# Gate of a feed-forward layer in pairs of blocks, by seven products of quarters

## The chip, the core and the metric

One core of a Trainium2 chip runs one program. The metric is the device time of one execution in microseconds, the median of several runs.

## The reference

Three transformer blocks in float32 on 256 tokens of 2048 features: two of a first kind (a state-space mixer beside latent attention, cross attention to a memory, feed-forward) and one hybrid block. What matters here is the feed-forward, with hidden width 5632:

```python
def swiglu(h, w_gate, w_up, w_down):
    return (jax.nn.silu(h @ w_gate) * (h @ w_up)) @ w_down
```

and the vector that shifts, scales and gates the hybrid block, a product of one row `c` with `w_ada` of 2048 x 6144:

```python
    ada = c @ w_ada + b_ada
    shift, scale, gate = jnp.split(ada, 3, axis=-1)
    h = rms_norm_2(x, g_pre) * (1.0 + scale[:, None, :]) + shift[:, None, :]
```

`shift` and `scale` are needed at the hybrid block's start, `gate` at its end.

## The kernel before, in words

Activations are kept feature-major as pairs of a high and a low part (`pair`, `hi_lo`, L348 to L370), four pairs of [128 features, 4 chunks, 256 tokens] for the 2048 features. A long product is computed in float32r as three matmuls: high x high, high x low of the weights, low x high (L423 to L425). `block` (L414) makes a token-major block of 512 columns: two PSUM banks of [128 tokens, 512], one for each token tile m, from the pool `psw` of four banks. Its weights come in half-tiles of [128, 2 chunks, 512], 512 KB each: `split` (L407) has SP load one into a `raw` buffer (five of them, L410), ACT copy it to `wh` (L411) and VectorE (DVE) subtract to get `wl` (L412). There are four `wh` and four `wl` buffers. A half-tile serves two chunks for both token tiles, 12 matmuls; the last half-tile of a block serves bank 0, then bank 1 (HOLD).

PE runs its instructions in the order in which the program is written; a scheduler orders those of the other engines by readiness and priority at build time, and each engine then runs its own in order. `early` (L316) and `weights` raise the priority. Work beside the long products is written as tasks (`spawn`, L265) that a `block` advances one step with every `tick` (L270), once for each chunk: the transposes of a hidden tile, attention heads and the like. A block of 2048 features has 15 ticks.

`ffn` (L1180) goes over 11 hidden blocks j of 512 columns in each of two layers: a gate block with Silu (L1188), an up block multiplied onto it (L1192), the transposes of the result as a task (L377, L358, L359), and the four down blocks of block j - 1, added to x by DVE (`x_add`, L485). In the second layer `ada` (L1234) then takes nine of 96 parts of `w_ada`: SP loads 512 KB into a slot, and DVE multiplies and sums it (L1240). `hybrid` (L1555) computes the last block, with four `ma` blocks beside which nothing else is loaded than their weights.

SBUF pools: `rawp` 5, `wp` 4, `xp` 6 pairs, and 72 KB a partition in `sp`, `k2`, `k1` for what tasks need. PSUM: four wide banks (`psw`) and four for the tasks (`psm`).

## Time and profile before

| | us |
|---|---|
| median of three runs | 3197.23 |
| lowest and highest run | 3197.22, 3197.4 |
| span of the profiled execution, first to last instruction | 3196.7 |
| first feed-forward stage | 454 to 1190 |
| second feed-forward stage | 1632 to 2360 |

The profile gives the span of the profiled execution; what lies around it, taken against the median, is 0.5 us. In the rows PE is TensorE's matmul queue, PEld its weight loads, DVE VectorE, ACT ScalarE, POOL GpSimd, SP the queue that issues most transfers. A matmul's record is longer than its spacing, since matmuls overlap.

### The profile page before, as it was taken

What the parts mean: (1) busy time and instruction counts of PE and PEld (TensorE: products, weight loads), DVE (VectorE), ACT (ScalarE), POOL (GpSimd) and SP (SyncE); (2) the same over time, 40 slices, a digit from 0 to 9 for tenths busy, and PEclk for the clock granted to TensorE, in tenths of its full rate; (3) what the DMA queues carried; (4) which work ended last, traced back from release to release, by engine and by line L of the source; (5) the groups of instructions that cost most, each with busy time, mean ns of one, the idle gap of its engine ahead of it and who ended that gap; (6) DMA issues with size and microseconds to landing.
All of it is one profiled execution on the core that took longest, in us unless ns stands there. A gap on an engine that the chain in (4) does not pass through costs nothing.

```text
span 3196.7 us, 41513 instructions
## 1 busy us (share of the span) xinstructions
PE 3175.3 (99%) x15705; PEld 2656.9 (83%) x15705; DVE 2034.1 (64%) x3015; ACT 1553.8 (49%) x2191; POOL 53.4 (2%) x77
## 2 busy tenths in 40 slices
PE   9999999999999999999999999999999999999998
PEld 8987888888888889887888888888878977888887
DVE  6886665555555566885767677766765555455554
ACT  7465564444444455474654444444454455444443
POOL 0010000000000000010000000000000000000000
PEclk9999999999999999999999999999999999999999
DMA  8554555555555556454567777777746533555454
GB/s 299 172 169 145 186 172 187 192 192 191 192 187 192 191 175 189 159 183 141 190 228 265 266 270 270 253 250 269 269 143 219 174 105 99 179 184 180 162 184 151
DMA packets 175160, 625.28 MB, mean 196 GB/s; under 512 B 19696, under 2 KB 19952, under 8 KB 174704
## 3 DMA queue, kind: packets, MB, share of 16 engines
q1 hardware_dynamic: 173952, 620.26, 58.2%
q8 instruction: 123, 2.02, 0.3%
q10 hardware_dynamic: 1008, 2.37, 0.2%
q14 instruction: 77, 0.63, 0.1%
HBM read 620.46 MB, written 2.10 MB: 195 GB/s over the span
## 4 chain that ended last, share of the span: by engine, by line
PE 96%; DVE 1%; DMA 1%; issue 1%; POOL 0%; ACT 0%; SPq 0%; DVEq 0%; POOLq 0%; ACTq 0%
PE pw L423 27%; PE pw L425 27%; PE pw L424 27%; PE pw L461 2%; PE pw L462 2%; PE pw L463 2%; PE mb L377 2%; PE mb L665 2%; DMA wada<-w_ada 1%; PE mb L1493 1%; PE mb L1346 0%; PE mb L903 0%; DVE wl L412 0%; PE mb L1496 0%; PE mb L887 0%
## 5 line engine op out<-in xcount | busy, mean ns | idle before, releaser
L412 DVE TENSOR_TENSOR wl<-raw,wh 128x1024 fp32r<-128x1024 f32 (+3 forms) x1069 | 1285.6, 1204 | 969.7 <-ACT wh L411 967.2
L411 ACT ACTIVATE wh<-raw 128x1024 fp32r<-128x1024 f32 (+3 forms) x1069 | 1114.9, 1043 | 1384.8 <-PE pw L425 1258.0
L423 PE MATMUL pw<-wh,xh 128*128 128x512 f32 (+2 forms) x3952 | 1555.4, 394 | 6.2 <-ACT wh L411 4.9
L425 PE MATMUL pw<-wh,xl 128*128 128x512 f32 (+2 forms) x3952 | 1526.3, 386 | 0.0
L424 PE MATMUL pw<-wl,xh 128*128 128x512 f32 (+2 forms) x3952 | 1524.6, 386 | 0.6 <-DVE wl L412 0.6
L423 PEld LDWEIGHTS pw<-wh,xh 128*128 128x128 f32 x3952 | 744.2, 188 | 153.3 <-ACT wh L411 4.9
L425 PEld LDWEIGHTS pw<-wh,xl 128*128 128x128 f32 x3952 | 743.1, 188 | 150.7 <-DVE xl L368 0.7
L424 PEld LDWEIGHTS pw<-wl,xh 128*128 128x128 f32 x3952 | 744.6, 188 | 141.6 <-DVE wl L412 2.1
L461 PE MATMUL pw<-xh,wh 128*128 128x256 f32 x640 | 183.2, 286 | 0.0
L463 PE MATMUL pw<-xh,wl 128*128 128x256 f32 x640 | 181.2, 283 | 0.0
L462 PE MATMUL pw<-xl,wh 128*128 128x256 f32 x640 | 181.1, 283 | 0.0
L485 DVE TENSOR_TENSOR x<-x,pw 128x512 f32<-128x512 f32 x224 | 144.9, 679 | 3.8 <-PE pw L425 3.8
L1240 DVE CUSTOM_DVE_ANT_0 wada<-wada,crow 128x1024 f32<-128x1024 f32 x96 | 117.3, 1221 | 33.9 <-DMA wada<-w_ada 33.8
L461 PEld LDWEIGHTS pw<-xh,wh 128*128 128x128 f32 x640 | 122.7, 192 | 1.3 <-issue 0.8
L462 PEld LDWEIGHTS pw<-xl,wh 128*128 128x128 f32 x640 | 122.8, 192 | 0.1
L463 PEld LDWEIGHTS pw<-xh,wl 128*128 128x128 f32 x640 | 122.7, 192 | 0.0
L630 ACT ACTIVATE t<-t,mn 128x256 f32<-128x256 f32 (+1 forms) x128 | 58.4, 457 | 63.1 <-DVE mn L627 62.3
L367 ACT ACTIVATE xh<-mb,par 128x256 fp32r<-128x256 f32 x112 | 50.9, 467 | 13.1 <-PE mb L377 12.2
L368 DVE SCALAR_TENSOR_TENSOR xl<-mb,par,xh 128x256 fp32r<-128x256 f32 x112 | 51.8, 478 | 3.7 <-ACT xh L367 2.6
L334 POOL TENSOR_TENSOR xr<-rs,mhalf 128x1 f32<-128x1 f32 x16 | 9.8, 619 | 2512.1 <-DVE rs L330 2306.4
L358 ACT ACTIVATE xh<-mb 128x512 fp32r<-128x512 f32 (+1 forms) x68 | 35.1, 516 | 30.5 <-PE mb L377 15.8
L627 DVE CUSTOM_DVE_ANT_0 t<-mb,cst 128x128 f32<-128x128 f32 x80 | 26.0, 354 | 25.8 <-PE mb L665 25.4
(358 smaller groups left out, 1564.4 us busy)
## 6 DMA issues: line engine op xcount, KB each, us to landing
raw<-w_gate SPq DMA_DIRECT2D x176, 512.0 KB, 3.6
raw<-w_up SPq DMA_DIRECT2D x176, 512.0 KB, 3.8
raw<-w_down SPq DMA_DIRECT2D x176, 512.0 KB, 3.6
raw<-w_out SPq DMA_DIRECT2D x96, 512.0 KB, 3.5
wada<-w_ada SPq DMA_DIRECT2D x96, 512.0 KB, 5.5
raw<-w_in_x SPq DMA_DIRECT2D x48, 512.0 KB, 3.9
raw<-w_in_z SPq DMA_DIRECT2D x32, 512.0 KB, 3.5
raw<-w_ma SPq DMA_DIRECT2D x32, 512.0 KB, 3.3
```

Source lines behind the costliest of these rows:

```text
L377: self.nc.tensor.transpose(t[:, j, m * P:(m + 1) * P], src(m), self.ident)
L411: nc.scalar.activation(h, raw, AF.Copy)
L412: nc.vector.tensor_tensor(l, raw, h.bitcast(F32), op=OP.subtract)
L423: nc.tensor.matmul(pt[m], lhsT=xh[:, k, ms], rhs=wh[:, j], start=c == 0, stop=False)
L424: nc.tensor.matmul(pt[m], lhsT=xh[:, k, ms], rhs=wl[:, j], start=False, stop=False)
L425: nc.tensor.matmul(pt[m], lhsT=xl[:, k, ms], rhs=wh[:, j], start=False, stop=c == 4 * n - 1)
L461: nc.tensor.matmul(pt, lhsT=h[:, j], rhs=xh[:, c], start=(k == 0), stop=False)
L462: nc.tensor.matmul(pt, lhsT=h[:, j], rhs=xl[:, c], start=False, stop=False)
L463: nc.tensor.matmul(pt, lhsT=l[:, j], rhs=xh[:, c], start=False, stop=(k == 15))
L485: self.nc.vector.tensor_tensor(xs, xs, pt[m], op=OP.add)
L665: nc.tensor.matmul(s[:, a:b], lhsT=q[:, m * P:(m + 1) * P], rhs=k[:, 0:b - a], start=(i == 0), stop=(i == len(parts) - 1))
L1240: nc.vector.tensor_tensor_reduce(out=t, in0=t, in1=self.crow[hf], scale=1.0, scalar=0.0, op0=OP.mult, op1=OP.add, accum_out=self.adap[:, j ...
```

## The change

Two gate blocks are computed together as a 2 x 2 by 2 x 2 product of quarters: the rows are the two token tiles, the contraction is the two halves of 1024 features, the columns are the two blocks. Seven products take the place of eight. Each has eight chunks of 128 features, for 128 tokens and 512 columns. The sums of activations are made once per layer (`x_sums`) and kept as high and low parts; the sums of weights are made anew for each pair: W00 + W01 and W11 + W01 by transfers from POOL that add to the tile in SBUF, the two later ones by additions on DVE. Block 0 is computed as before, blocks 1 to 10 in five pairs. A task, `gate_pair`, has 28 steps of one half-tile and six matmuls each, spread over 48 or 64 ticks of the two up blocks of the pair and the down blocks of the pair before. Down takes two hidden blocks in one PSUM accumulation.

The pools `sp`, `k2`, `k1` are closed for the feed-forward and give place to 70 KB a partition of others: `fs` (sums of activations, 8), `fr` (gate weights, 5), `fu` (up, 2), `fe` (temporaries, 4), `fc` (a row of `c`, 1). Each pair keeps one wide PSUM bank and up to three of the others.

`w_ada` is read in 96 transfers of two half rows into `raw` buffers: 7 at the start of each layer's feed-forward, 6 (first layer) or 4 (second) beside each pair, the last third, needed only for `gate`, beside the `ma` blocks of the hybrid block.

```diff
-    o["c_rows"] = np.ascontiguousarray(_rows(a["c_2"][0])).reshape(P, 2, 1024)
-    o["w_ada"] = np.ascontiguousarray(a["w_ada_2"][0].T).reshape(48, P, 2, 1024)
+    o["c_rows"] = np.ascontiguousarray(_rows(a["c_2"][0])).reshape(P, 4, 512)
+    w = a["w_ada_2"][0].T.reshape(24, 2, P, 4, 512)
+    o["w_ada"] = np.ascontiguousarray(w.transpose(0, 3, 2, 1, 4))
...
         self.tasks = []
         pool = lambda name, bufs, **k: ctx.enter_context(tc.tile_pool(name=name, bufs=bufs, **k))
         self.one = pool("one", 1)
+        self.sm = pool("sm", 1)
         self.rawp = pool("rawp", 5)
         self.wp = pool("wp", 4)
         self.xp = pool("xp", 6)
-        self.sp = pool("sp", NSLOT)
-        self.k2 = pool("k2", NT2)
-        self.k1 = pool("k1", NT1)
-        self.sm = pool("sm", 1)
         self.psw = pool("psw", 4, space=PSUM)
         self.psm = pool("psm", 4, space=PSUM)
+        self.scope = ctx.enter_context(ExitStack())
+        self.open_main()
         ctx.enter_context(tc.manual_schedule(engines={mybir.EngineType.PE}))
...
+    def part(self, **bufs):
+        self.scope.close()
+        for name, n in bufs.items():
+            setattr(self, name, self.scope.enter_context(self.tc.tile_pool(name=name, bufs=n, reuse_waits="tile")))
+    def open_main(self):
+        self.part(sp=NSLOT, k2=NT2, k1=NT1)
+    def open_ffn(self):
+        self.part(fs=8, fr=5, fu=2, fe=4, fc=1)
...
+    def half(self):
+        return self.fe.tile([P, 512], F32, name="fe", tag="fe")
+    def x_sums(self, pairs):
+        nc = self.nc
+        for t in pairs:
+            if isinstance(t, _Task):
+                yield from self.after(t)
+        prs = [self.get(t) for t in pairs]
+        S = [[self.fs.tile([P, 8, P], F32R, name="fs", tag="fs") for _ in range(2)] for _ in range(4)]
+        for i in range(2):
+            def quarter(k, m):
+                return [t[:, :, m * P:(m + 1) * P].bitcast(F32) for t in prs[2 * k + i]]
+            (h11, l11), (h12, l12), (h21, l21), (h22, l22) = (quarter(k, m) for m in range(2) for k in range(2))
+            def tmp():
+                return self.half().rearrange("p (a b) -> p a b", a=4)
+            flat = lambda t: t.rearrange("p a b -> p (a b)")
+            def put(n, t, sign=1.0):
+                h, l = (x[:, i * 4:i * 4 + 4] for x in S[n])
+                nc.scalar.activation(h, t, AF.Copy, scale=sign)
+                nc.vector.scalar_tensor_tensor(flat(l), flat(t), sign, flat(h.bitcast(F32)),
+                                               op0=OP.mult, op1=OP.subtract)
+            a, b = tmp(), tmp()
+            nc.vector.tensor_tensor(a, h21, h22, op=OP.subtract)
+            nc.vector.tensor_tensor(b, l21, l22, op=OP.subtract)
+            nc.vector.tensor_tensor(a, a, b, op=OP.add)
+            put(0, a, -1.0)
+            nc.vector.tensor_tensor(b, a, h11, op=OP.subtract)
+            nc.vector.tensor_tensor(b, b, l11, op=OP.subtract)
+            put(1, b)
+            c = tmp()
+            nc.vector.tensor_tensor(c, h12, b, op=OP.add)
+            nc.vector.tensor_tensor(c, c, l12, op=OP.add)
+            put(3, c, -1.0)
+            a, b = tmp(), tmp()
+            nc.vector.tensor_tensor(a, h11, h21, op=OP.subtract)
+            nc.vector.tensor_tensor(b, l11, l21, op=OP.subtract)
+            nc.vector.tensor_tensor(a, a, b, op=OP.add)
+            put(2, a)
+            yield 2
+        return S
+    def gate_pair(self, pairs, sums, srcs, r, u, ticks):
+        nc = self.nc
+        S = yield from self.after(sums)
+        pr = [self.get(t) for t in pairs]
+        def quarter(k, m):
+            return lambda c: [t[:, c % 4, m * P:(m + 1) * P] for t in pr[2 * k + c // 4]]
+        def total(n):
+            return lambda c: [t[:, c] for t in S[n]]
+        def load(k, n, q, t=None):
+            src = srcs[n][2 * k + q // 2][q % 2]
+            with self.early():
+                if t is None:
+                    t = self.fr.tile([P, 2, 512], F32, name="fr", tag="fr")
+                    nc.sync.dma_start(t, src)
+                else:
+                    nc.gpsimd.dma_start(t, src, accum_op=OP.add)
+            return t
+        def product(bank, x, t, q, first, last):
+            with self.early():
+                h = self.wp.tile([P, 2, 512], F32R, name="wh", tag="wh")
+                l = self.wp.tile([P, 2, 512], F32R, name="wl", tag="wl")
+                nc.scalar.activation(h, t, AF.Copy)
+                nc.vector.tensor_tensor(l, t, h.bitcast(F32), op=OP.subtract)
+            for j in range(2):
+                xh, xl = x(2 * q + j)
+                g = not first
+                nc.tensor.matmul(bank, lhsT=xh, rhs=h[:, j], start=first and q == 0 and j == 0, stop=False,
+                                 skip_group_check=g)
+                nc.tensor.matmul(bank, lhsT=xh, rhs=l[:, j], start=False, stop=False, skip_group_check=g)
+                nc.tensor.matmul(bank, lhsT=xl, rhs=h[:, j], start=False, stop=last and q == 3 and j == 1,
+                                 skip_group_check=g)
+        def gated(t, n, m, r=r):
+            while len(u) <= n:
+                yield 1
+            with self.early():
+                nc.scalar.activation(t, t, AF.Silu, scale=r[:, m:m + 1])
+                nc.vector.tensor_tensor(u[n][:, m], u[n][:, m], t, op=OP.mult)
+        def add(t, x):
+            with self.early():
+                nc.vector.tensor_tensor(t, t, x, op=OP.add)
+        done = [0]
+        def step():
+            done[0] += 1
+            return done[0] * ticks // 28 - (done[0] - 1) * ticks // 28
+        ba, bb, bd = self.wbank([P, 512]), self.bank([P, 512]), self.bank([P, 512])
+        ws = []
+        for q in range(4):
+            ws.append(load(0, 0, q))
+            product(ba, quarter(0, 0), ws[q], q, True, True)
+            load(0, 1, q, ws[q])
+            yield step()
+        for q in range(4):
+            product(bb, quarter(1, 0), load(1, 0, q), q, True, True)
+            yield step()
+        for q in range(4):
+            product(bd, total(0), ws[q], q, True, True)
+            yield step()
+        with self.early():
+            t1, t5 = self.half(), self.half()
+            nc.scalar.activation(t1, ba, AF.Copy)
+            nc.vector.tensor_tensor(t1, t1, bb, op=OP.add)
+            nc.scalar.activation(t5, bd, AF.Copy)
+        gate_1 = self.spawn(gated(t1, 0, 0), 1)
+        bc, be = self.bank([P, 512]), self.bank([P, 512])
+        for g in (0, 2):
+            a, b = {}, {}
+            for q in (g, g + 1):
+                a[q] = load(1, 1, q)
+                product(bd, total(3), a[q], q, False, True)
+                load(0, 1, q, a[q])
+                yield step()
+            for q in (g, g + 1):
+                product(bc, total(2), a[q], q, True, True)
+                b[q] = load(0, 0, q)
+                add(b[q], a[q])
+                yield step()
+            for q in (g, g + 1):
+                product(ba, total(1), b[q], q, False, True)
+                a[q] = load(1, 0, q)
+                add(a[q], b[q])
+                yield step()
+            for q in (g, g + 1):
+                product(be, quarter(1, 1), a[q], q, True, True)
+                yield step()
+        with self.early():
+            nr = self.small([P, 2], name="nr", bufs=1)
+            nc.vector.tensor_scalar(nr, r, -1.0, None, op0=OP.mult)
+            t2, t3 = self.half(), self.half()
+            nc.scalar.activation(t2, ba, AF.Copy)
+            nc.vector.tensor_tensor(t3, t2, bd, op=OP.add)
+            nc.vector.tensor_tensor(t2, t2, bc, op=OP.add)
+            nc.vector.tensor_tensor(t5, t2, t5, op=OP.add)
+            nc.vector.tensor_tensor(t2, t2, be, op=OP.add)
+        yield from gated(t3, 1, 0, nr)
+        yield from gated(t5, 1, 1, nr)
+        yield from gated(t2, 0, 1)
+        yield from self.after(gate_1)
     def ffn(self, l, pairs, r):
         nc, I = self.nc, self.I
         parts = self.x_parts()
-        def hidden(j):
-            s = self.slot([P, 2, 512], "ff")
-            pt = self.block(pairs, I["w_gate"][l, j])
+        last = l == DEPTH - 1
+        self.open_ffn()
+        self.crow = None
+        sums = self.spawn(self.x_sums(pairs), 1)
+        def up(j):
+            pt = self.block(pairs, I["w_up"][l, j])
+            s = self.fu.tile([P, 2, 512], F32, name="fu", tag="fu")
             for m in range(2):
-                nc.scalar.activation(s[:, m], pt[m], AF.Silu, scale=r[:, m:m + 1])
+                with self.early():
+                    nc.scalar.activation(s[:, m], pt[m], AF.Identity, scale=r[:, m:m + 1])
+            return s
+        def hidden(s, delay, first=None):
+            def steps():
+                if first is not None:
+                    yield from self.after(first)
+                return (yield from self.transposed(lambda m: s[:, m]))
+            return self.spawn(steps(), delay)
+        def down(js, hs):
+            for nb in range(4):
+                self.x_add(nb, self.block(list(hs), [I["w_down"][l, nb, j] for j in js]))
+                self.tick()
+        self.spawn(self.ada_steps(7, 4), 2)
+        s = up(0)
+        pt = self.block(pairs, I["w_gate"][l, 0])
+        for m in range(2):
+            t = self.half()
+            with self.early():
+                nc.scalar.activation(t, pt[m], AF.Silu, scale=r[:, m:m + 1])
+                nc.vector.tensor_tensor(s[:, m], s[:, m], t, op=OP.mult)
+        prev = [0], [hidden(s, 2)]
+        for js in ([1, 2], [3, 4], [5, 6], [7, 8], [9, 10]):
+            end = js[1] == NH_FFN - 1
+            u = []
+            srcs = [I["w_gate"][l, j] for j in js]
+            gate = self.spawn(self.gate_pair(pairs, sums, srcs, r, u, 48 if js[0] == 1 or end else 64), 1)
+            self.spawn(self.ada_steps(6 if l == 0 else 4, 8), 4)
+            for j in js:
+                u.append(up(j))
+            hs = [hidden(s, 1 + 4 * i, gate) for i, s in enumerate(u)] if end else None
+            down(*prev)
+            self.get(gate)
+            prev = js, hs or [hidden(s, 1 + 4 * i) for i, s in enumerate(u)]
+        js, hs = prev
+        if last:
+            self.ada_end()
+        out = []
+        for nb in range(4):
+            pt = self.block(hs, [I["w_down"][l, nb, j] for j in js])
+            if nb == 0:
+                self.open_main()
+            if nb == 3:
+                with self.tc.high_priority(offset=2 * HP):
+                    self.x_add(nb, pt, parts)
+                    r = self.x_rms(parts)
+            else:
+                self.x_add(nb, pt, parts)
+            out.append(self.spawn(self.x_fm(nb), 2) if last else self.x_pair(nb, self.p(f"{l + 1}.attn_g")))
             self.tick()
...
-    def ada_start(self):
-        nc = self.nc
...
-    def ada(self, n):
-        nc = self.nc
-        for i in self.ada_left[:n]:
-            j, hf = i // 2, i % 2
-            t = self.slot([P, 1024], "wada")
-            nc.sync.dma_start(t, self.I["w_ada"][j, :, hf])
-            nc.vector.tensor_tensor_reduce(
-                out=t, in0=t, in1=self.crow[hf], scale=1.0, scalar=0.0, op0=OP.mult, op1=OP.add,
-                accum_out=self.adap[:, j, hf:hf + 1])
+        return out, r
+    def ada(self, n, pool=None):
+        nc = self.nc
+        for k, i in self.ada_left[:n]:
+            if self.crow is None or self.crow[0] != k:
+                t = self.fc.tile([P, 512], F32, name="crow", tag="fc") if pool is None else pool([P, 512])
+                nc.sync.dma_start(t, self.I["c_rows"][:, k])
+                self.crow = k, t
+            t = self.rawp.tile([P, 2, 512], F32, name="raw", tag="raw")
+            nc.sync.dma_start(t, self.I["w_ada"][i, k])
+            for h in range(2):
+                nc.vector.tensor_tensor_reduce(
+                    out=t[:, h], in0=t[:, h], in1=self.crow[1], scale=1.0, scalar=0.0, op0=OP.mult, op1=OP.add,
+                    accum_out=self.adap[:, 2 * i + h, k:k + 1])
         self.ada_left = self.ada_left[n:]
+    def ada_steps(self, n, every, pool=None):
+        for _ in range(n):
+            with self.early():
+                self.ada(1, pool)
+            yield every
+    def ada_sum(self, lo, hi):
+        nc = self.nc
+        c = self.adac[:, lo:hi]
+        for t in [self.adap[:, lo:hi, k] for k in (1, 2, 3)] + [self.p("b_ada")[:, lo:hi]]:
+            nc.vector.tensor_tensor(c, c, t, op=OP.add)
     def ada_end(self):
         nc = self.nc
-        self.ada(96)
-        self.adac = self.one.tile([P, 48], F32, name="adac")
-        nc.vector.tensor_tensor(self.adac, self.adap[:, :, 0], self.adap[:, :, 1], op=OP.add)
-        nc.vector.tensor_tensor(self.adac, self.adac, self.p("b_ada"), op=OP.add)
+        self.ada(len(self.ada_left))
+        self.ada_sum(0, 32)
         self.g2 = self.one.tile([P, 16], F32, name="g2")
         nc.vector.scalar_tensor_tensor(self.g2, self.adac[:, 16:32], 1.0, self.p("g_pre"), op0=OP.add, op1=OP.mult)
+        self.ada_left = [(k, i) for k in range(4) for i in range(16, 24)]
...
+        self.crow = None
+        ada = self.spawn(self.ada_steps(32, 2, self.t2), 1)
...
+        self.get(ada)
         gr = self.spawn(self.gate_rows(), 2)
...
     def run(self):
-        self.ada_left = []
+        self.adap = self.one.tile([P, 48, 4], F32, name="adap")
+        self.adac = self.adap[:, :, 0]
+        self.crow = None
+        self.ada_left = [(k, i) for k in range(4) for i in range(16)]
         pairs, r = self.start(), None
         for l in range(DEPTH):
             pairs, r, kt = self.mixer(l, pairs, r)
             pairs, r = self.cross(l, pairs, r, kt)
-            if l == DEPTH - 1:
-                self.ada_start()
             pairs, r = self.ffn(l, pairs, r)
         self.hybrid(pairs, r)
```

## Rows read from the trace of the kernel before

**Rows 1.** The page's first part: busy us (share of the span) xinstructions, by engine.

```profile
span 3196.7 us, 41513 instructions
PE 3175.3 (99%) x15705; PEld 2656.9 (83%) x15705; DVE 2034.1 (64%) x3015; ACT 1553.8 (49%) x2191; POOL 53.4 (2%) x77
```

**Rows 2.** Windows by stage: us, PE, PEld, DVE, ACT, POOL busy (count), PEclk, DMA share, GB/s.

```profile
454.00:1190.00 736.00, 736.00 (x3309) 609.68 (x3309) 414.33 (x427) 321.58 (x350) 1.66 (x3) 1.00 0.58 190
...
1632.00:2360.00 728.00, 727.72 (x3266) 602.47 (x3265) 511.36 (x600) 315.64 (x335) 2.17 (x2) 1.00 0.75 259
```

**Rows 3.** Waits of the whole span: waiter, released by: us in total, times, longest.

```profile
ACT wh L411 <- PE pw L425: 1258.0, 868, 3.9
...
PE pw L423 <- ACT wh L411: 4.9, 1, 4.9
```

**Rows 4.** Timeline of PE in the first feed-forward: start, duration, instruction.

```profile
575.66 0.39 PE L424 MATMUL pw<-wl,xh 128*128 128x512 f32 x1
575.89 0.39 PE L425 MATMUL pw<-wh,xl 128*128 128x512 f32 x1
...
583.82 0.39 PE L424 MATMUL pw<-wl,xh 128*128 128x512 f32 x1
```

**Rows 5.** Groups by line and form, 454 to 1190 us: busy, mean ns, idle.

```profile
L412 DVE TENSOR_TENSOR wl<-raw,wh 128x1024 fp32r<-128x1024 f32 x265 | 324.7, 1225 | 321.0 <-ACT wh L411 320.4
L411 ACT ACTIVATE wh<-raw 128x1024 fp32r<-128x1024 f32 x266 | 282.4, 1062 | 400.8 <-PE pw L425 400.8
L485 DVE TENSOR_TENSOR x<-x,pw 128x512 f32<-128x512 f32 x90 | 58.4, 679 | 0.0
```

**Rows 6.** Timeline of DVE in the second feed-forward.

```profile
1899.24 1.23 DVE L412 TENSOR_TENSOR wl<-raw,wh 128x1024 fp32r<-128x1024 f32 x1 [1.50 <-ACT wh L411]
1900.39 1.22 DVE L1240 CUSTOM_DVE_ANT_0 wada<-wada,crow 128x1024 f32<-128x1024 f32 x1
```

**Rows 7.** Windows inside the second feed-forward.

```profile
1780.00:1800.00 20.00, 20.00 (x94) 16.56 (x93) 17.89 (x25) 8.54 (x10) 0.00 (x0) 1.00 0.86 307
```

**Rows 8.** DMA, first feed-forward, then second (GB/s in 40 slices), then w_ada: us to landing.

```profile
raw<-w_up SPq DMA_DIRECT2D x86, 512.0 KB, 3.5
...
GB/s 173 287 338 231 345 305 203 198 340 309 195 209 318 296 222 217 325 306 194 227 310 310 203 216 326 308 202 223 292 275 245 233 323 300 188 237 310 300 196 245
...
wada<-w_ada SPq DMA_DIRECT2D x93, 512.0 KB, 5.5
raw<-w_up SPq DMA_DIRECT2D x88, 512.0 KB, 4.3
...
DMA to landing us min/median/max: 4.4/5.5/9.1
```

**Rows 9.** Timelines of DVE, SP and ACT around 700 us; in brackets the idle time before.

```profile
699.65 1.23 DVE L412 TENSOR_TENSOR wl<-raw,wh 128x1024 fp32r<-128x1024 f32 x1 [0.30 <-ACT wh L411]
...
700.90 3.05 SPq L410 DMA_DIRECT2D raw<-w_up  x2
...
701.28 1.06 ACT L411 ACTIVATE wh<-raw 128x1024 fp32r<-128x1024 f32 x1 [1.66 <-PE pw L425]
```

**Rows 10.** Windows beside the ma blocks of the last stage.

```profile
2720.00:2760.00 40.00, 40.00 (x195) 33.48 (x193) 17.90 (x17) 16.53 (x18) 0.00 (x0) 1.00 0.55 182
2760.00:2800.00 40.00, 40.00 (x179) 33.12 (x178) 17.58 (x16) 18.11 (x19) 0.00 (x0) 1.00 0.57 189
```

42 lines of the change are left out of this document (4 added, 38 removed).

## The prediction

> **What bounds the kernel now.** I read the page's first part, the windows by stage, the waits, then single instructions. TensorE (PE) is busy 3175.3 of 3196.7 us [rows 1]; in both feed-forward stages, 454 to 1190 and 1632 to 2360 us, it is idle for 0.3 us together, at full granted clock [rows 2]. What PE is waiting for is nearly nothing: ACT's split waits for PE 1258 us in all, and PE for ACT 4.9 us [rows 3]. So only fewer matmuls, or a new PE wait, move the end. VectorE (DVE) and the DMA engines have room, but not the same everywhere: DVE is at 56% in the first feed-forward and at 70% in the second, where `w_ada` is read, and DMA is at 58% and 75% [rows 2].
>
> A matmul record lasts 0.39 us, but they overlap; the price is the spacing: 575.66 to 583.82 us holds 36 steps, 0.227 us each [rows 4]. A group of six (one weight chunk for two token tiles, or in the change one weight half-tile for one token tile twice) is 1.36 us.
>
> **The change, part by part.**
>
> *Matmuls removed.* Two gate blocks take 2 x 16 chunks x 2 token tiles x 3 = 192 matmuls; seven products take 7 x 8 x 3 = 168. Five pairs in each of two layers: 10 x 24 = 240 fewer, at 0.227 us, 54.4 us off a PE that is never idle there. Up and down keep their matmuls; block 0's gate too.
>
> *Weight tiles added.* A pair's gate needs 28 splits instead of 16. Each is 1.06 us on ACT and 1.225 us on DVE [rows 5], spaced 1.15 us when DVE runs back to back [rows 6]. Per pair (two gate, two up, two down blocks, PE about 133 us now, 127 then) DVE gets 60 x 1.15 = 69 us of splits, 8 sums of weights at the price of a split, the nearest row, 9 us, 8 instead of 16 additions to x at 0.68 [rows 5] = 5 us, some 13 operations of 128x512 at 0.68 to evict, combine and multiply = 9 us, the hidden tiles' low parts 3 us, and up to 12 half reductions of `w_ada` at half of 1.22 us [rows 6] plus a read, 8 us: 103 us or 81%. ACT has 60 x 1.06 + 9 = 73 us, 57%. Neither is the bound on average. Between 1780 and 1800 us DVE was at 89%, DMA at 0.86 and 307 GB/s, and PE lost nothing [rows 7]. I cost this at nothing; if the cover goes, it shows as DVE's splits coming late.
>
> *Sums of activations.* 28 operations of 128x512 on DVE per layer, 0.68 us each = 19 us, and 16 copies on ACT, at the stage's start beside 16 splits and 7 reductions, about 50 us of DVE in 43 us of PE; the rest spills into the first pair, where the first total is needed some 34 us later. Between 0 and 7 us a layer; I take 1, so 2 in all, since DVE has about 15 us left in that time.
>
> *Accumulating transfers.* 80 in all, issued by POOL after both readers of the tile (ACT, DVE) are done. Behind each, POOL's queue holds only the next ones; PE, through ACT and DVE, waits for it. The four of the first phase have eight steps before use. In the second phase a tile is split at one step and its sum two steps later: 8.6 us of PE work at the slow pace (64 ticks), 7.4 at the fast one (48). With the lookahead worked out below (4.5 us, less a second split of 2.3) such a transfer may take 10.8 or 9.6 us from DVE's end. The trace has none. The nearest rows are the plain transfers of the same size: 3.5 us in the quiet layer, 4.3 and 5.5 beside `w_ada`, 9.1 at most [rows 8]. At any of these it costs nothing; at twice 9.1, 18 us, some 8 us twice in each pair, 160 us. I take 5.5 to 8 us, nearest the loaded rows, and nothing.
>
> *Five buffers for the gate's tiles (fr).* In the first phase four of them hold tiles that are being summed until steps 9 to 12, so the four tiles of steps 5 to 8 go one after the other through the fifth. SP can load the next only when DVE has split the last; SP does issue at once (DVE ends at 700.88, SP starts at 700.90) [rows 9]. One round is C = landing + 1.06 + 1.23 + waiting in ACT's and DVE's queues. Behind SP's waiting load stand the raw tiles for up, five deep. From step 5 to step 8 PE has 11 groups of work at 64 ticks (7 ticks, one of them with two groups at the seam of two blocks, and 3 gate steps), 15.0 us; at 48 ticks 9 groups, 12.2 us. How early is a split? ACT starts it the moment PE frees one of the four wh buffers [rows 9]; five groups, 6.8 us, lie between that and its use, so 6.8 - 2.3 = 4.5 us of lookahead. The stall per pair is 3C - 15.0 - 4.5, or 3C - 12.2 - 4.5, never below nothing. With three slow and two fast pairs per layer:
> - landing 3.5, no waiting, C = 5.8: 0 and 0.7 a pair, 3 us in all;
> - landing 4.3 and 0.3 of waiting, C = 6.9: 1.2 and 4.0, 23 us;
> - landing 5.5 and 0.3, C = 8.1: 4.8 and 7.6, 59 us; with an instruction ahead on DVE (1.2), C = 9.0: 86 us.
> I take 23: the traffic will be like that beside `w_ada` (66 transfers of 0.524 MB per 127 us = 272 GB/s, against 259 in the second layer now [rows 2]), and the 4.3 is a raw load's median there.
>
> *`w_ada` moved.* Of 96 transfers 37 go to the first layer, 27 to the second, 32 beside the four ma blocks of the last stage. From the second layer nothing is gained, since PE lost nothing there. Beside ma the load is now 182 to 189 GB/s, DVE at 45% [rows 10]; 32 more in 64 ticks (92 us) add 16.8 MB, 182 GB/s, and DVE 32 x 1.4 = 45 us. That is 370 GB/s; the busiest slice seen is 345 [rows 8]. 33.6 MB at 345 is 97 us: 5 us lost. Bounds: 0, and 20 if the five raw buffers, now shared by both streams, turn over in 8.3 us rather than 7. The `c_rows` loads (a few, 256 KB) and SP's 12 additional issues less 8 on POOL, 0.33 us each, lie beside this.
>
> *PSUM.* ba keeps one of four wide banks for a whole pair, so a block's second bank is the last block's first, freed by an eviction of 0.68 us that has a group and a half (2 us) of cover: nothing.
>
> **Sum:** -54.4 + 23 + 5 + 2 + 0 = -24 us. From the span of 3196.7, 3172.3; the median, 3197.23, is 0.5 us above the span, so 3173 us.
>
> **A rule weighed against the trace.** Per pair the DMA share by the rows is 272/307 x 0.86 = 0.76, with every transfer counted once. The Trainium skill, "Collectives: The Full Stack", section "The bandwidth ceiling", says of the add in the DMA engines that it needs two source reads, two descriptors on the same read ring, so that a reduce moves half as fast as a copy. By that rule 8 of a pair's 66 transfers count twice, and the share is an estimated 0.85, still under what PE bore without loss; no run here shows it yet.
>
> **The rivals.**
> 1. *The chain is covered* (landing 3.5 to 4). For it: the first layer's median is 3.5. Against: 43% more bytes there. Cost 3 to 5, with 5 beside ma: about 3150. Chance 0.20.
> 2. *Accumulating transfers take twice a loaded one*, 11 us. Then the sum is late by 0.2 us at the slow pace and 1.4 at the fast one, twice a pair: 2 x 2 x (3 x 0.2 + 2 x 1.4) = 14 us, and their traffic lifts the chain to C = 7.1, 29 us: -54 + 14 + 29 + 7 = -4, 3193. Chance 0.12. It is that rule of the Trainium skill, "Collectives: The Full Stack", on the add's two reads, that would give this.
> 3. *Slower: the fifth fr buffer.* One mechanism: steps 5 to 8 of each pair go load, split, load, split. Cost in all 30C - 184 us; it eats the gain, less 7, at C = 7.7, a landing of 5.1 with 0.3 of waiting. At the 5.5 that `w_ada`'s transfers took, 59: 3211; with a DVE instruction ahead each time, 3238. For it: bursts will be worse than the mean, and DVE is fuller. Against: raw loads beside `w_ada` had 4.3. Chance 0.30.
> 4. *The change doesn't do what it says*: DVE's or ACT's order lets the splits for up wait behind a late gate tile, and PE loses as much as the 240 matmuls give and more. Against: 1780 to 1800 us. Chance 0.02, slower.
>
> The forecast, 3160 to 3188, has 0.36.
>
> **Numbers.** About 0.2%, 6.4 us, is what a measurement here can tell from nothing. Faster: 0.36 + 0.20 = 0.56; same: rival 2, 0.12; slower: 0.32. The range for 8 in 10 goes from 3145, nearly the whole 54 us, to 3228, in rival 3 between its two prices. Cases of both signs have most of it; the likeliest one's own range is 3160 to 3188.
>
> **What would show it.** Right: 240 fewer 512-column matmuls; PE idle of some 20 to 30 us in the feed-forward stages, in pieces of 1 to 4 us about a third into each pair, ended by ACT's or DVE's split, that wait for an fr landing; more of it in the first and last pair of a layer; SP waiting for DVE's split there. DVE near 80% in both stages. Beside ma, DMA at 0.9 or more. Wrong: PE idle ended by tiles that POOL's transfers wrote (rival 2), landing over 5 us (rival 3), the granted clock at 1.2 GHz behind such a piece, or PE idle spread evenly, which would make DVE the bound.

## The result, and the profile after

The changed kernel takes 3309.4 us in the median of 4 runs (3303.1 to 3311.1), the kernel before 3197.2: 1.0345 times as long, 95% interval 1.0331 to 1.036. The forecast was 3173 in a range of 3145 to 3228: the sign was wrong, and the miss is 136 us. The profiled run's span is 3301.3 us at a mean granted clock of 0.988; before it was 3196.7 at 0.998.

First the page's first part and its DMA queues, the answer to [rows 1].

```profile
span 3301.3 us, 42150 instructions
PE 3175.1 (96%) x15465; PEld 2625.0 (80%) x15465; DVE 2275.5 (69%) x3449; ACT 1723.5 (52%) x2401; POOL 124.3 (4%) x157
...
q1 hardware_dynamic: 180720, 642.55, 55.8%
q0 software_dynamic: 11520, 41.95, 7.4%
...
PE 61%; DMA 15%; DVE 11%; issue 8%; ACT 3%; POOL 1%; SPq 0%; DVEq 0%; ACTq 0%; POOLq 0%
```

The 240 matmuls are gone, and PE is busy for as long as before: matmuls that follow a stop run slower. PE's idle time, span less busy time, is 126.2 us and was 21.4. PE has 61% of the chain that ended last. POOL's queue, q0, moves 6.5% of the bytes of q1 and takes 13% of its engine time.

Now the windows of both feed-forward stages, which answer to [rows 2].

```profile
461.00:1243.00 782.00, 729.16 (x3177) 590.38 (x3177) 569.12 (x676) 404.45 (x450) 37.27 (x43) 0.98 0.76 238
1690.00:2467.00 777.00, 729.56 (x3164) 590.17 (x3162) 552.41 (x626) 404.34 (x451) 36.75 (x43) 0.98 0.75 233
```

The stages are 46 and 49 us longer than before [rows 2], where 27 fewer each were to be had. Yet nothing is full: DVE has 73% and 71%, ACT 52%, DMA 0.76. So the loss is in waits. Those of PE over the whole span, then those for transfers; they answer to [rows 3], where PE's longest row was 4.9 us.

```profile
PE pw L437 <- DVE x L499: 37.6, 10, 8.0
PE mb L1278 <- DVE wl L1272: 18.0, 20, 2.4
PE mb L1276 <- ACT wh L1271: 14.6, 13, 4.1
PE mb L391 <- DVE fu L1287: 14.2, 10, 2.9
PE pw L437 <- ACT fu L1366: 7.7, 6, 1.4
PE pw L438 <- DVE wl L426: 7.4, 13, 1.4
...
ACT wh L1271 <- DMA fr<-w_gate: 147.7, 40, 7.8
...
DVE fr L1291 <- DMA fr<-w_gate: 75.1, 42, 3.8
DVE raw L1434 <- DMA raw<-w_ada: 54.2, 44, 3.3
```

The six rows of PE are 99.5 us in 72 stops. L437 to L439 are the matmuls of an ordinary block, L1276 to L1279 those of the seven products. L499 is the addition to x behind a down block; L1271, L1272 are the gate's splits, L1287 the multiplication by the gate, L1366 the eviction of an up block, L391 the transposes, L426 the ordinary split, L1291 an addition of weights, L1434 the multiplication of `w_ada`. The clock is a second loss. The share of the span at 1.2 GHz, worked out as twice what the mean clock lacks of 1, is 2.4% after (79 us) and 0.4% before (13 us); a matmul there takes nearly twice as long (a spacing of 0.43 us, shown below, instead of 0.227), so about 33 us more than before. As an estimate, 99.5 + 33, some 12 us for 72 restarts (a record of 0.39 us instead of a spacing of 0.227), and 9.6 us that the control below gives to the frame make 154, against the 159 to be explained (104.6 by the spans, 54.4 by the matmuls).

The first kind of stop, in the first pair: SP's loads through the fifth fr buffer, ACT's waits for them, and PE (timeline: start, duration, instruction, idle before it and what ended it).

```profile
518.04 0.33 SPq L1262 DMA_DIRECT2D fr<-w_gate  x1
527.96 0.33 SPq L1262 DMA_DIRECT2D fr<-w_gate  x1
533.84 0.33 SPq L1262 DMA_DIRECT2D fr<-w_gate  x1
...
525.62 1.06 ACT L1271 ACTIVATE wh<-fr 128x1024 fp32r<-128x1024 f32 x1 [6.32 <-DMA fr<-w_gate]
...
526.73 0.49 PE L1276 MATMUL mb<-wh,xh 128*128 128x512 f32 x1 [2.63 <-ACT wh L1271]
527.99 0.50 PE L1278 MATMUL mb<-wl,xh 128*128 128x512 f32 x1 [0.77 <-DVE wl L1272]
```

That is the chain load, split, load, split that the prediction had. The first round, from 518.04 to 527.96 us, takes 9.9 us: its load lands after 7.5 us, beside two of POOL's adding transfers. The next takes 5.9 us (527.96 to 533.84), less than the 6.9 assumed. In the mean of the ten pairs the three rounds take 21.5 us together, and PE stands still for 34.1 us in all of them (26.4 before L1276 and L1278, 7.7 before L437 for the eviction L1366).

The second kind, and the longest, is in the same pair's second phase: DVE, then PE.

```profile
599.84 2.36 DVE L1291 TENSOR_TENSOR fr<-fr 128x1024 f32<-128x1024 f32 x2 [1.14 <-DMA fr<-w_gate]
602.12 1.22 DVE L1272 TENSOR_TENSOR wl<-fr,wh 128x1024 fp32r<-128x1024 f32 x1
603.25 1.22 DVE L426 TENSOR_TENSOR wl<-raw,wh 128x1024 fp32r<-128x1024 f32 x1
604.39 1.22 DVE L1272 TENSOR_TENSOR wl<-fr,wh 128x1024 fp32r<-128x1024 f32 x1
605.52 1.22 DVE L1291 TENSOR_TENSOR fr<-fr 128x1024 f32<-128x1024 f32 x1
606.66 1.87 DVE L499 TENSOR_TENSOR x<-x,pw 128x512 f32<-128x512 f32 x3
...
607.48 0.77 PE L437 MATMUL pw<-wh,xh 128*128 128x512 f32 x1 [8.04 <-DVE x L499]
608.05 0.63 PE L438 MATMUL pw<-wl,xh 128*128 128x512 f32 x1
608.47 0.63 PE L439 MATMUL pw<-wh,xl 128*128 128x512 f32 x1
```

PE's last matmul before this began at 599.05. It wants a PSUM bank that an addition of 0.68 us would free. The additions to x have ordinary priority, and stand in DVE's queue behind early additions of weights and splits. Some of these had waited for transfers (1.14 us just before 599.84); from 599.84 on it is 6.8 us of work without a pause. Behind the stop the spacing is 0.43 us, and the granted clock is 0.50, the lower level (the window from 607.40 to 611.00 us):

```profile
607.40:611.00 3.60, 3.52 (x8) 2.81 (x9) 2.45 (x6) 0.00 (x0) 0.00 (x0) 0.50 0.53 204
```

### The profile page after: what moved, and what is told of

It reads as the page before. It is cut to its first block, busy times and chain, and to the rows that moved or that the text cites. A ratio compares the mean times of both kernels' runs of the same rounds, so it can differ in the third digit from the quotient of the medians.

```text
span 3301.3 us, 42150 instructions
## 1 busy us (share of the span) xinstructions
PE 3175.1 (96%) x15465; PEld 2625.0 (80%) x15465; DVE 2275.5 (69%) x3449; ACT 1723.5 (52%) x2401; POOL 124.3 (4%) x157
## 3 DMA queue, kind: packets, MB, share of 16 engines
q0 software_dynamic: 11520, 41.95, 7.4%
## 4 chain that ended last, share of the span: by engine, by line
PE 61%; DMA 15%; DVE 11%; issue 8%; ACT 3%; POOL 1%; SPq 0%; DVEq 0%; ACTq 0%; POOLq 0%
PE pw L437 15%; PE pw L439 14%; PE pw L438 14%; DMA fr<-w_gate 9%; DVE wl L426 3%; DVE wl L1272 3%; DMA raw<-w_ada 3%; PE pw L475 2%; PE pw L477 2%; PE pw L476 2%; PE mb L679 2%; PE mb L391 2%; DMA raw<-w_ma 2%; ACT wh L1271 1%; ACT wh L425 1%
## 5 line engine op out<-in xcount | busy, mean ns | idle before, releaser
L426 DVE TENSOR_TENSOR wl<-raw,wh 128x1024 fp32r<-128x1024 f32 (+3 forms) x909 | 1088.1, 1199 | 567.9 <-ACT wh L425 556.9
L425 ACT ACTIVATE wh<-raw 128x1024 fp32r<-128x1024 f32 (+3 forms) x909 | 943.3, 1038 | 949.7 <-PE pw L439 596.4
L437 PE MATMUL pw<-wh,xh 128*128 128x512 f32 (+2 forms) x3312 | 1314.6, 397 | 51.0 <-DVE x L499 37.6
L438 PE MATMUL pw<-wl,xh 128*128 128x512 f32 (+2 forms) x3312 | 1286.1, 388 | 7.7 <-DVE wl L426 7.4
L439 PE MATMUL pw<-wh,xl 128*128 128x512 f32 (+2 forms) x3312 | 1284.3, 388 | 0.0
L437 PEld LDWEIGHTS pw<-wh,xh 128*128 128x128 f32 x3312 | 629.1, 190 | 183.5 <-DVE x L499 33.8
L438 PEld LDWEIGHTS pw<-wl,xh 128*128 128x128 f32 x3312 | 629.5, 190 | 133.8 <-DVE wl L426 16.7
L439 PEld LDWEIGHTS pw<-wh,xl 128*128 128x128 f32 x3312 | 627.8, 190 | 127.4 <-DVE xl L382 0.7
L1271 ACT ACTIVATE wh<-fr 128x1024 fp32r<-128x1024 f32 x280 | 296.3, 1060 | 306.7 <-DMA fr<-w_gate 147.7
L1272 DVE TENSOR_TENSOR wl<-fr,wh 128x1024 fp32r<-128x1024 f32 x280 | 341.6, 1221 | 161.6 <-ACT wh L1271 156.6
L1291 DVE TENSOR_TENSOR fr<-fr 128x1024 f32<-128x1024 f32 x80 | 97.6, 1223 | 75.5 <-DMA fr<-w_gate 75.1
L1434 DVE CUSTOM_DVE_ANT_0 raw<-raw,crow 128x512 f32<-128x512 f32 x128 | 85.8, 688 | 53.7 <-DMA raw<-w_ada 53.4
L1278 PE MATMUL mb<-wl,fs 128*128 128x512 f32 x240 | 94.7, 395 | 6.3 <-DVE wl L1272 6.2
L499 DVE TENSOR_TENSOR x<-x,pw 128x512 f32<-128x512 f32 x144 | 95.2, 679 | 3.1 <-PE pw L439 3.1
L1279 PE MATMUL mb<-wh,fs 128*128 128x512 f32 x240 | 93.9, 391 | 0.0
```

The lines of the kernel that those rows point to most:

```text
L425: nc.scalar.activation(h, raw, AF.Copy)
L426: nc.vector.tensor_tensor(l, raw, h.bitcast(F32), op=OP.subtract)
L437: nc.tensor.matmul(pt[m], lhsT=xh[:, k, ms], rhs=wh[:, j], start=c == 0, stop=False)
L438: nc.tensor.matmul(pt[m], lhsT=xh[:, k, ms], rhs=wl[:, j], start=False, stop=False)
L439: nc.tensor.matmul(pt[m], lhsT=xl[:, k, ms], rhs=wh[:, j], start=False, stop=c == 4 * n - 1)
L499: self.nc.vector.tensor_tensor(xs, xs, pt[m], op=OP.add)
```

## The experiments

Times are of one run each unless more are named; the kernel before gave 3197.6 to 3200.3 beside them. The changed kernel's four runs span 8 us, so differences under that are not read. The first phase of a pair is its first 12 steps, the second the other 16.

**The chain of bb's four tiles.** The four steps of the product in bank `bb`, which need no summed tile, go ahead of the four that keep their tiles.

```diff
         ws = []
+        for q in range(4):
+            product(bb, quarter(1, 0), load(1, 0, q), q, True, True)
+            yield step()
         for q in range(4):
             ws.append(load(0, 0, q))
...
-        for q in range(4):
-            product(bb, quarter(1, 0), load(1, 0, q), q, True, True)
-            yield step()
```

> Edit: the four steps of the product with W10 (plain loads, each tile free after its split) come before the four steps whose tiles stay for the sum, so that no four tiles are held while four others pass through the fifth fr buffer. Theory A (ACT and DVE stand in order behind a gate tile that comes late; one source of late tiles is the fifth fr buffer in the first phase, the other the accumulating transfers in the second): the waits of the first phase, about 16 us of listed PE idle a layer, go, with the half clock behind them: 30 to 50 us less than the changed kernel's 3309, so 3260 to 3280. Rival B (DVE's work as a whole bounds the feed-forward, 551 of 760 us busy): nothing moves, 3300 to 3315. Rival C (the add in the DMA engines takes their time): nothing moves either.

Measured: 3254.2, 49 to 57 us less than the changed kernel's runs and 6 below the range expected. The stops before L1276 are gone. Between the two profiled runs PE's idle time falls by 27.6 us and its busy time by 21.3. So the chain is real. In idle time it cost about 28 us for a term of 23; with the slower matmuls behind the stops, twice its term. The additions to x still stop PE for 36.8 us.

**The adding transfers, first try.** In the second phase a plain load and an addition on DVE take the place of each adding transfer.

```diff
-                load(0, 1, q, a[q])
+                b[q] = load(0, 1, q)
+                add(b[q], a[q])
+                a[q] = b[q]
```

> Edit: in the second phase the 40 accumulating transfers become plain loads into another fr buffer, added on DVE (40 more additions of 1.15 us, 46 us of DVE work). Theory A: the sums no longer wait for a transfer that can only start after the split before; listed PE idle of the second phase, about 29 us a layer, goes, with the half clock behind it: 60 to 90 us less, 3220 to 3250. Rival B: 20 to 46 us more, 3330 to 3355. Rival C: half of the adds leave the DMA engines; DMA share falls by about 0.03, 20 to 40 us less.

Measured: 3280.2, 23 to 31 us less: not the 60 to 90 of A, not slower as B had it, but within the 20 to 40 of C, by which the adds take the DMA engines' time.

> Edit: e1 and e2 together; the first phase keeps its accumulating transfers, used four steps after they start. Theory A: both sources of late tiles go, what stays is the end of each pair (hidden's transposes wait for the last gated tile, 7 us a layer) and a few waits for w_ada: 90 to 140 us less than 3309, 3170 to 3220. Rival B: 20 to 46 us more than 3309. Rival C: as e2, 3270 to 3290.

With both edits: 3266.6, worse than the chain's repair alone. Additions to x stop PE for 35.1 us in 16, ordinary splits for 20.3 in 25. Two gains that don't add up suggested one thing behind them, DVE's order. Next, the price of the add itself; this kernel leaves the sums out:

```diff
-                    nc.gpsimd.dma_start(t, src, accum_op=OP.add)
+                    nc.gpsimd.dma_start(t, src)
```

> Edit: the transfers from POOL stay where they are, with the same waits, but copy instead of adding, so the sums W00 + W01 and W11 + W01 are left out and the result is another. Theory A: what costs is that the transfer starts only after the split and is waited for two steps later; issue to landing stays near 6.7 us less whatever the add costs, and the time stays within 20 us of 3309. Rival C: landing falls to the 4.7 us of SP's fr loads, DMA share of the feed-forward falls from 0.77 to about 0.72, and 40 us or more go. Rival B: 3309.

Measured: 3237.9, 71 us less than the median. The transfers by issuer (count, size, median us to landing) and q0, first with adding, then copying:

```profile
fr<-w_gate SPq DMA_DIRECT2D x200, 512.0 KB, 4.7
...
fr<-w_gate POOLq DMA_DIRECT2D x80, 512.0 KB, 6.7
```

```profile
fr<-w_gate SPq DMA_DIRECT2D x200, 512.0 KB, 4.7
fr<-w_gate POOLq DMA_DIRECT2D x80, 512.0 KB, 4.5
...
q0 software_dynamic: 11520, 41.95, 4.1%
```

An add lands 2.2 us later than a copy from the same queue and takes 1.8 times the engines' time (7.4% and 4.1% for the same bytes). So C's landing and time are borne out, against A's "within 20 us of 3309"; the DMA share of the pairs hardly fell, from 0.79 to 0.78, as the transfers fill less time. By the Trainium skill's "Collectives: The Full Stack", section "The bandwidth ceiling", the add needs two source reads and so twice a copy's descriptors. In engine time these rows come near that, 1.8; their packet counts, 11520 in both, don't show the second read. Part of the 71 us is the chain of the first phase: beside copies its first load lands after 5.1 us in the mean of the ten pairs, beside adds after 7.2, and PE's idle time in the three rounds is 20.3 us instead of 34.1. But in the first layer's first and last pair 7 us stops for the additions to x stay even so (7.00 at 602.76 us); DVE works without a pause from 595.11 us until that addition, so this one is order, not transfer.

**Order.** Additions to x early; then with bb first; then also the transposes of a pair's two hidden tiles four and eight ticks after its end instead of one and five (not in a layer's last pair, where they are started elsewhere); then bb first and the later transposes, without the early additions.

```diff
-                self.x_add(nb, self.block(list(hs), [I["w_down"][l, nb, j] for j in js]))
+                pt = self.block(list(hs), [I["w_down"][l, nb, j] for j in js])
+                with self.early():
+                    self.x_add(nb, pt)
...
-            prev = js, hs or [hidden(s, 1 + 4 * i) for i, s in enumerate(u)]
+            prev = js, hs or [hidden(s, 4 + 4 * i) for i, s in enumerate(u)]
```

> The changed kernel, with the additions to x in the down blocks given the same early priority as the gate's splits and sums; nothing else moves. Theory A (order on DVE): the two wide PSUM banks of a down block wait for an addition that stands in DVE's queue behind splits and sums that are themselves waiting for transfers; with the addition ahead of them the stops of PE that x_add ends (37.6 us in 10, longest 8.0) go, and with them some of the half-clock stretches behind them: 3245 to 3265. Rival (DVE's throughput, or the transfers, are the limit): the same idle time comes back in front of DVE's splits: 3290 to 3311, stops ended by wl longer by 25 us or more.

> The four steps of bb first, and the additions to x early. Theory A: the two repairs add up, 3254 less the 36.8 us of x_add stops less some 10 us of half clock: 3195 to 3215. Rival: 3235 to 3255, the time stays and only the row that ends the stops changes.

> The one before, and the transposes of the hidden tiles start four ticks after the end of a pair instead of one, so that PE doesn't meet them before the last multiplication by the gate. Theory A: the stops in front of the transposes (15.2 us in all) go: 12 to 20 us below the one before, so 3177 to 3200. Rival (that time is DVE's lag and comes back at the next split): within 5 us of the one before.

> The four steps of bb first, and the transposes of the hidden tiles four ticks after a pair's end; the additions to x keep their low priority. It splits the 39 us that the later transposes gave when the additions were early. Theory A (the two stops at a pair's end stand in for each other: a DVE that is behind is met either at the addition to x or at the transposes, so both have to go): the x_add stops stay (30 us or more) and the time falls little below 3254: 3235 to 3250. Rival (the transposes alone were the stop that counted): below 3225.

Measured: 3291.4, 3253.8, 3215.1 and 3237.1. Raising the additions alone gives 12 to 20 us, and beside bb first nothing: theory A fell for these two, and the rivals' times held. As they had it, other rows take the stop over: with the additions alone early, that of the transposes goes from 14.2 to 30.4 us and that of the ordinary splits from 7.4 to 21.8. PE's first waits with bb first and additions early:

```profile
PE mb L391 <- DVE fu L1287: 29.6, 10, 5.7
PE pw L438 <- DVE wl L426: 26.2, 26, 4.0
```

The addition is no longer met late; the chain at a pair's end is. It is an eviction, four combinations, and three times Silu and a multiplication, alternating between ACT and DVE, and PE wants the result one tick after the last product. DVE in that kernel, at the end of the first pair (L1344 to L1347 combine the products):

```profile
615.28 0.68 DVE L1345 TENSOR_TENSOR fe<-fe,mb 128x512 f32<-128x512 f32 x1
615.88 1.22 DVE L1272 TENSOR_TENSOR wl<-fr,wh 128x1024 fp32r<-128x1024 f32 x1
617.01 0.69 DVE L1346 TENSOR_TENSOR fe<-fe 128x512 f32<-128x512 f32 x1
617.61 1.22 DVE L426 TENSOR_TENSOR wl<-raw,wh 128x1024 fp32r<-128x1024 f32 x1
618.75 0.69 DVE L1287 TENSOR_TENSOR fu<-fu,fe 128x512 f32<-128x512 f32 x1
619.35 0.68 DVE L1347 TENSOR_TENSOR fe<-fe,mb 128x512 f32<-128x512 f32 x1
619.95 1.22 DVE L1272 TENSOR_TENSOR wl<-fr,wh 128x1024 fp32r<-128x1024 f32 x1
621.08 0.69 DVE L1287 TENSOR_TENSOR fu<-fu,fe 128x512 f32<-128x512 f32 x1
```

The seven operations of the chain on DVE, 0.7 us each, take from 611.75 to 621.77 us, since splits and additions to x stand between them. PE stands still from 616.1 to 621.8. Later transposes take that away, and give 39 us with the additions early, 17 without (there the additions to x stop PE for 39.7 us): the two stops stand in for each other. A DVE that is behind is met at the first thing PE wants of it. With the three repairs DVE has the same work as in the changed kernel, 2275.5 us there, and the time is 94 us less:

```profile
PE 3145.3 (98%) x15465; PEld 2609.0 (81%) x15465; DVE 2272.8 (71%) x3449; ACT 1725.2 (54%) x2401; POOL 123.1 (4%) x157
```

**The frame.** Up and gate as ordinary blocks, in pairs, `w_ada` where the change put it.

```diff
-            gate = self.spawn(self.gate_pair(pairs, sums, srcs, r, u, 48 if js[0] == 1 or end else 64), 1)
...
+                pt = self.block(pairs, I["w_gate"][l, j])
```

> The frame of the change without the seven products: up and the gate as ordinary blocks, down in pairs, w_ada beside ma, no sums of activations or weights and no transfers by POOL. It has the 240 matmuls again. Theory A (the seven products and their order cost the time): the frame costs what the last stage lost, 3 us, and little more: 3198 to 3210. Rival (pairing down, the shared raw buffers or w_ada's steps stop PE): over 3230.

Measured: 3207.9, so the frame costs 9.6 and the seven products the rest. In the frame's trace `w_ada`'s early multiplications stand between the last additions to x of the stage ahead. The last of these starts 3.8 us later than before in the first layer (458.65 instead of 454.88 us), and the second layer adds as much again. Beside the ma blocks the frame loses 3.3 us, the changed kernel 4.6: the matmuls that took from 2770.51 to 2880.32 us before take from 2869.30 to 2983.69 there.

**What is left, with order repaired (3215).** Six fr buffers for one fe buffer; `w_ada` multiplied three ticks after its load (the edit is the last one below, with a lag of 3); all of POOL's transfers copying, which leaves the sums out.

```diff
-        self.part(fs=8, fr=5, fu=2, fe=4, fc=1)
+        self.part(fs=8, fr=6, fu=2, fe=3, fc=1)
```

> All three repairs of order (bb first, additions to x early, transposes later: 3215), and six fr buffers instead of five, paid for with one of the four fe buffers. Theory A (in the second phase too the ring of the gate's tiles makes loads start late, so DVE meets an add whose transfer hasn't landed, 78 us of such waits): those waits fall by half, 3190 to 3205. Rival (one buffer isn't what delays the loads; the chain through the accumulating transfer is): within 5 us of 3215.

> The three repairs of order (3215), and the multiplication by c of each w_ada tile issued three ticks after its load instead of at once. Theory A (DVE works in order, so each wait for w_ada's landing, 74 us in 54, delays the splits behind it): 3195 to 3208. Rival (these waits fall into time that DVE has, or the raw ring, one tile fuller, gives the time back): 3210 to 3222.

> The three repairs of order (3215), and POOL's 80 transfers copy instead of adding, so the products that should take W00+W01 and W11+W01 take W01 alone. It prices the adding itself without the stops of order. Theory A (after the repairs PE still waits for sums that land 2 us later than plain loads, and the transfers take twice the engines' time): 25 us or more below, 3170 to 3190, nearly all that the 240 matmuls give against the frame of 3208. Rival (the 71 us that copying gave before was order, which the repairs have taken): 3205 to 3215.

Measured: 3222.7, 3217.1 and 3170.3. Neither buffers nor a short lag help; the adding costs 45 us. Where it does, and what can be done about it. First, only the second phase's transfers copy, and its sums go without W11:

```diff
...
-                load(0, 1, q, a[q])
+                load(0, 1, q, a[q], OP.bypass)
```

> The three repairs of order (3215), with only the second phase's 40 transfers by POOL copying instead of adding; it leaves out W11 in the sums W11+W01 and W11+W01+W00, and the first phase's sum stays. Theory A (lateness: sums that are used two steps after they are issued hold up ACT and DVE): nearly all of the 45 us of full copying, 3170 to 3185. Rival (traffic: each adding transfer takes twice the engines' time wherever it stands): half of it, 3188 to 3200.

> The three repairs of order, and the second phase's sums W11+W01 by a plain load and VectorE, as in the earlier experiment that gave 3280 before the repairs. Theory A (lateness of the sums is the larger part): 3190 to 3210. Rival (the plain loads need the same five fr buffers and DVE 46 us more, so DVE is late by more than the transfers were): 3215 to 3235.

Then the second phase adds on DVE, as in the first try. Last, it goes in four runs of four steps, and POOL makes all sums:

```diff
-        for g in (0, 2):
...
+        for q in range(4):
+            a.append(load(1, 1, q))
+            product(bd, total(3), a[q], q, False, True)
+            load(0, 1, q, a[q])
+            yield step()
+        for q in range(4):
+            product(bc, total(2), a[q], q, True, True)
+            load(0, 0, q, a[q])
+            yield step()
+        for q in range(4):
+            product(ba, total(1), a[q], q, False, True)
+            load(1, 0, q, a[q])
+            yield step()
...
```

> The three repairs of order, and the second phase in four runs of four steps instead of two groups of eight: all four tiles are summed in place by POOL, W11, +W01, +W00, +W10, so each adding transfer has four steps and not two, and VectorE adds no weights. The adding transfers go from 80 to 160 and the loads fall by 80. Theory A (lateness): no sum is late any more and DVE has 92 us less to do: 3165 to 3190. Rival (traffic): 3.8% more of the 16 engines' time, landings over 9 us, 3215 to 3250.

Measured: 3170.8, 3213.1 and 3196.5. Copying in the second phase alone gives all of the 45: the first phase's 40 adding transfers, which with bb first have four steps and no longer eight, cost nothing here. The second phase's, which have two, cost it all. Additions on DVE are no cheaper. With four steps each, twice as many adding transfers are 18.6 us *better*, so their traffic alone is not the cost; this edit also takes 81 us of work off DVE, so it doesn't show lateness by itself. It missed its 3165 to 3190. Its longest stop shows a reason (DVE, SP, PE):

```profile
699.97 0.69 DVE L1433 CUSTOM_DVE_ANT_0 raw<-raw,crow 128x512 f32<-128x512 f32 x1 [8.94 <-DMA raw<-w_ada]
...
688.91 0.33 SPq L1431 DMA_DIRECT2D raw<-w_ada  x1
...
701.86 0.80 PE L438 MATMUL pw<-wl,xh 128*128 128x512 f32 x1 [4.80 <-DVE wl L426]
```

A `w_ada` load takes 11.1 us from its issue to its use, DVE waits for it in its order, and the half of a split for which ACT was done at 692.5 us stands behind. Two remedies, one in ten runs and one in four:

```diff
-            self.spawn(self.ada_steps(6 if l == 0 else 4, 8), 4)
+            self.spawn(self.ada_steps(6 if l == 0 else 4, 4), 4)
```

> The kernel with four summed tiles (3196.5), with w_ada's loads every four ticks instead of every eight, so that they fall mostly into a pair's first phase, where POOL has four adding transfers and not twelve. Theory A (DVE waits in its order for w_ada tiles that land late beside adding transfers): the stops of 3 to 5 us of PE go, 3175 to 3188. Rival (the traffic is the same over a pair, the waits move into the first phase): 3192 to 3200.

```diff
         for _ in range(n):
             with self.early():
                 self.ada(1, pool)
-            yield every
+            late, w = self.late, min(LAG, every - 1)
+            yield w
+            with self.early():
+                self.ada_reduce(*late)
+            yield every - w
...
```

> The kernel with four summed tiles (3196.5), with w_ada's loads where they were and the multiplication by c issued five ticks behind each load. Theory A (it is only DVE's in-order wait): 3178 to 3190. Rival (the tile is held longer in the five raw buffers, so SP's next loads start later and the splits for up and down wait instead, as the lag of three ticks gave nothing before): 3193 to 3205.

Measured: 3197.6 (3191.9 to 3207.5), ratio to the kernel before 1.0003 (0.9993 to 1.0012), and, with a lag of five ticks, **3183.4** (3178.5 to 3187.1), **ratio 0.995 (0.9934 to 0.9967)**. Where the loads lie made no difference. The lag gave 9 to 18 us against the one run of 3196.5, but its edit does less than it says: PE, ACT, SP and POOL run the same instructions in the same order as without it, and on DVE only six of `w_ada`'s 128 multiplications in the two feed-forwards have moved: each has changed places with a multiplication by the gate that stood a little behind it. Of the waits, the 1.2 to 3.3 us that DVE had spent before each of these six are gone, 11.8 us together. The others stay, without the lag and with it, and PE still stops behind them (2.96 us at 825.96):

```profile
DVE raw L1433 <- DMA raw<-w_ada: 103.5, 50, 8.9
```

```profile
DVE raw L1441 <- DMA raw<-w_ada: 88.8, 46, 7.1
...
824.07 0.69 DVE L1441 CUSTOM_DVE_ANT_0 raw<-raw,crow 128x512 f32<-128x512 f32 x1 [7.09 <-DMA raw<-w_ada]
```

The lag of three ticks had taken six such waits away too, 10.9 us, and the time stayed. So the in-order wait is shown at single stops; that it is what kept this kernel above 3190 is not, and why the lag gave something here and nothing there stays open. This last version, all repairs together, is 0.5% faster than the kernel before, a small difference but clear of 1 by its interval. Its page, and PE's first waits (lines stand one lower here):

```profile
span 3185.1 us, 42153 instructions
PE 3136.7 (98%) x15465; PEld 2615.3 (82%) x15465; DVE 2192.8 (69%) x3369; ACT 1726.9 (54%) x2401; POOL 193.0 (6%) x237
...
PE mb L1279 <- DVE wl L1273: 9.1, 4, 3.2
PE pw L439 <- DVE wl L427: 8.8, 8, 3.0
```

Against the frame (3207.9) the seven products are now worth 24 of 54 us. The other 30 were not pursued; some of it is the stops above, most of them in the first and last pairs, at 48 ticks.

## Why the prediction was wrong

The steps that failed are those at nothing: DVE's order, and the adding transfers that depend on it. The runs go from 3309.4 over 3254.2 (bb first) and 3215.1 (additions and transposes) to 3170.3 (copies): 55, 39 and 45 us, where the sum had 23, 0 and 0.

- *Matmuls removed, -54.4:* the count was right, 240, and so was the price, since the spacing stays 0.227 where PE doesn't stop. It is never all seen: with copies in place of adds 37.6 of it shows against the frame (3170.3 and 3207.9).
- *Splits, DVE's load, 0:* this is the step that failed first. DVE was costed as a sum of durations against a span (81%), and one window at 89% without loss [rows 7] was taken as proof. DVE came out lower, at 73%, and late all the same. It works in order, and its queue now holds instructions that wait for transfers (129 us in the two rows above), with PE's splits and additions behind them. In the window of [rows 7] four multiplications of `w_ada` stood in the queue too, but only one waited, for 0.16 us; in the whole kernel before these waits are:

```profile
DVE wada L1240 <- DMA wada<-w_ada: 33.8, 50, 3.4
```

- *PSUM bank and additions to x, 0:* wrong. "Two us of cover" was reckoned from the addition's duration, not from its place in the queue: 37.6 us of stops. That place alone, though, was worth only 12 to 20 us.
- *The end of a pair:* not in the sum. A pair's 13 operations were counted as DVE's load, and those at its end not as a chain that PE meets one tick later: 14.2 us in the changed kernel, 29.6 when other stops were gone. The later transposes were worth 39 us beside early additions, 17 without.
- *Accumulating transfers, 0:* the landing, 5.5 to 8, was right (6.7). The allowance of 10.8 or 9.6 us was not: POOL starts when DVE's split ends, and DVE ran late. ACT waited 3.65 us for a sum issued at 588.50, which landed in 6.1. Rival 2 had the place, a sum that comes late in the second phase, and 14 us, but for a landing of 11; with the landing at 6.7 it cost 45. That lateness is the reason and not the transfers' share of the engines is argued from the two steps against four, not shown by itself.
- *Fifth fr buffer, 23:* right in mechanism, undersized. PE stood still for 34.1 us. Three rounds took 21.5 us in the mean instead of 3 x 6.9 = 20.7, the first long (a landing of 4.6 to 9.0 us) and the others 5.9. The lookahead was about 2 us in the first pair instead of 4.5, since DVE's split of the tile before (516.80 to 518.02) came just ahead of its use by PE at 519.9. What was left out is what follows a stop: taking the chain away was worth 49 to 57.
- *`w_ada`, 5:* right, 4.6 beside the ma blocks. The cost ahead of each feed-forward was not seen; the in-order waits for it were left out.
- *Sums of activations, 2:* about right; no stop of over 1 us stands between the stage's start and the first pair's chain, where they lie (ACT's copies are 8 a layer, not 16).
- *The clock:* named as a sign, with no term. As estimated above, about 33 us.
- *The rule on the add's two reads*, the Trainium skill's "Collectives: The Full Stack", section "The bandwidth ceiling", was weighed by the DMA share alone. That stayed at 0.76, but at 238 GB/s and not at 272. The engine time was 1.8 times a copy's, and what counted was the landing, where there was no slack.
- *Rivals:* the slower side had 0.32, nearly all on the fr buffer. Rival 4, an order that costs more than the matmuls give, is nearest to what happened, and had 0.02. Rival 3's two prices, 3211 and 3238, come to 3209 and 3236 by its own terms, and two steps at the slow pace are 8.9 us by 64 ticks over 28 steps, not 8.6; neither changes a sign.

With order repaired and copies in place of the sums the kernel takes 3170, beside the 3173 forecast. That agreement is chance: this kernel has no chain through the fifth buffer, and without its 23 the sum gives 3150. Some 20 us are missing from it even where the engines meet on time, and the frame's 9.6, of which the sum had 5, is part of them.

## What to carry to other kernels

An engine's busy share says nothing about when PE gets its operand: for each new instruction in an in-order queue ask what it waits for and what PE needs from behind it. Cost cover from the instruction's place in its queue, not from its duration. A transfer that starts only after a compute engine has read its tile inherits that engine's delay, so give it several steps. Whether it pays to let a consumer come to its load later, rather than stand waiting for it, is open: it gave nothing once and 9 to 18 us once.

## What was not expected of the hardware

For 512 KB from POOL's queue an adding transfer landed 2.2 us after a copy (6.7 and 4.5 in the median) and took 1.8 times the engines' share. It slowed a neighbour where the median over all loads doesn't show it: SP's fr loads had a median of 4.7 us in both cases, while the one issued beside two adding transfers in each pair took 7.2 us in the mean, 5.1 beside copies. And the stretches at the lower clock all lie at or just behind stops of PE of 0.9 to 8.0 us in the changed kernel, but for the one at its very end. That is part of why the same 15465 matmuls were busy 3175 us in the changed kernel and 3137 in the last one.
